# Hybrid decoder layer on one core: up products with a 512-column moving operand, retention in plain fp32, the residual brought to token layout by VectorE and HBM

## The chip, the cores and the metric

The kernel runs on one core of a Trainium2 chip. The metric is device time in microseconds, from start to end of one execution. Inputs lie in HBM in float32; the weights alone are some 200 MB, and each of them is read once. The core has TensorE (PE, with its weight loads listed apart as PEld), VectorE (DVE), ScalarE (ACT), GpSimd (POOL) and SyncE (SP), whose queue issues nearly all DMAs.

## The reference

One layer works on 272 tokens (16 learned ones ahead of 256 of the input) with 2048 features:

```python
u = rmsnorm(h, attn_norm)
aq, ak, av, rq, rk, rv, rg = split(u @ w_in)      # 48 blocks of 128 columns
ya = rmsnorm(diff_attention(aq, ak, av))          # 8 heads
yr = rmsnorm(retention(rq, rk, rv)) * silu(rg)    # 4 heads, head size 256
h = h + concat(ya, yr) @ w_out                    # 16 blocks of 128
u = rmsnorm(h, ffn_norm)
g = u @ w_gate                                    # 44 blocks of 128
h = h + (silu(conv3(g)) * (u @ w_up)) @ w_down    # causal convolution over 3 tokens
out = rmsnorm(h, final_norm)[16:]
```

Retention here is, for each head, a masked and decayed score matrix times the values: `y = (q k^T * decay) v`. All of it is wanted to about float32 accuracy.

## The kernel before

**Layout.** Up to the last product, activations are kept transposed: features on the 128 partitions, tokens along the free axis. A product takes a 128x128 block of a weight matrix as the stationary operand and the tokens of one feature block as the moving operand; 16 feature blocks add up in one PSUM bank.

**High and low parts.** TensorE reads fp32r operands at reduced precision, so each float32 operand is kept as two fp32r tiles: the rounded high part and the rest. A product is three matmuls per block (lines 276 to 278): weight high with activation high, weight high with activation low, weight low with activation high. Each has its own weight load.

**Stages, in order.** A start stage does the first 4 column blocks of `w_in`; then come the other 44 (`gemm`, L257), with attention and retention tasks put between their matmuls by `pump`; then 16 blocks of `w_out` (loop at L550); then 44 pairs of gate and up blocks (loop at L587); then `w_down`, where the roles change: activations are stationary and 512 columns of the weight are the moving operand (L629 to L631). A gate block has 258 tokens (two more for the convolution), an up block 256.

**Weights.** `ahead` (L103) runs before each half block. `load` (L85) issues a 1 MB DMA on the SP queue into one of 3 `raw` tiles; `prep` (L90) makes the high part of half a block on ACT (L99) and the low part on DVE (L100), into 3 buffers each. A load waits until the block three places back has been prepared.

**Order.** The program is written in the order of the text, and a planner that simulates a timeline puts each engine's instructions in its own order. Each engine's queue, and each DMA queue, then runs strictly in that order.

**Retention** (`ret_tasks`, L401). `scores` (L415) multiplies k by q in plain fp32 (L420; one fp32 matmul shows as two records), applies the decay (L422), and splits the result into `sd` and `sl` (L423, L424). `vtr` (L428) transposes the values and splits them into `vh` and `vl` (L434, L435). `av` (L439) makes, for each of 2 value halves and 3 key blocks, three fp32r matmuls (L448 to L450) with 258, 172 and 86 columns.

**The w_out stage** (L550 to L574). For each block j a part of x is loaded (`xres`, L553), added to the product (`hT`, L556), squared and summed (L561, L562), and weighted and split into `ghi` and `glo` (L563, L564) for the next stage. `htr` (L567) brings `hT` to token layout for the residual of the last stage: two TensorE transposes (L570) into PSUM and one copy by ACT (L571) into `htok`.

**The gate and up stage** (L587 to L606). Gate: scale by `rstd2` (L590), convolve on DVE (L592, L595), SiLU on ACT (L598). Up: scale by `rstd2` (L601), multiply with the gate (L602), split into `fhi` (L603) and `flo` (L604). At its end POOL issues the load of `fn` (L611), which DVE scales once (L616), and three more buffers for weight halves are taken from the tiles of the activations (L608, L609).

Of the kernel before, what the change touches and what calls it, by code (L numbers as in the profile page):

```python
# [10 lines left out]
F32 = mybir.dt.float32  # L11
F32R = mybir.dt.float32r
# [7 lines left out]
P = 128  # L20
# [23 lines left out]
class Halves:  # L44
    def __init__(self, tiles):
        self.tiles = tiles

    def __getitem__(self, ix):
        p, k = ix[0], ix[1]
        return self.tiles[k // HK][(p, k % HK) + tuple(ix[2:])]  # L50
# [3 lines left out]
def trunk_kernel(ctx, tc, a, out):  # L54
# [6 lines left out]
    sp = ctx.enter_context(tc.tile_pool(name="small", bufs=2))  # L61

    xhi = Halves([big.tile([P, HK, T], F32R, tag=f"acthi{i}", name=f"xhi{i}")
                  for i in range(2)])
    xlo = big.tile([P, KT, T], F32R, tag="actlo", name="xlo")
# [191 lines left out]
    def gemm(idx, hi, lo, t0, n, pumps):  # L257
        if idx < 4:
            return first[idx]
        if idx < 6:  # L260
            ps = misc(f"mm{idx}")
        elif idx == 6:
            ps = psx[:, 1]
        else:
            ps = ps1.tile([P, 512], F32, tag="mm", bufs=3, name=f"mm{idx}")
        for half in range(2):
            hf = 2 * idx + half
            ahead(hf)
            whi, wlo = pairs.pop(hf)
            for kk in range(HK):  # L270
                k = half * HK + kk
                wh = whi[:, kk * P:(kk + 1) * P]
                wl = wlo[:, kk * P:(kk + 1) * P]
                xh = hi[:, k, t0:t0 + n]
                xl = lo[:, k, t0:t0 + n]
                PE.matmul(ps[:, :n], wh, xh, start=(k == 0), stop=False)  # L276
                PE.matmul(ps[:, :n], wh, xl, start=False, stop=False)  # L277
                PE.matmul(ps[:, :n], wl, xh, start=False, stop=(k == KT - 1))  # L278
                if kk == HK // 2 - 1 or kk == HK - 1:
                    pump(pumps)  # L280
        return ps

    with ExitStack() as p1:
# [118 lines left out]
        def ret_tasks(r, k, q, vs):  # L402
# [4 lines left out]
            sd = [ap_.tile([P, (3 - j) * QT], F32R, tag=f"at{j}", name=f"sd{r}_{j}")  # L407
                  for j in range(3)]
            sl = [ap_.tile([P, (3 - j) * QT], F32R, tag=f"sl{j}", name=f"sl{r}_{j}")
                  for j in range(3)]  # L410
            vh = ap_.tile([P, 3, 2 * P], F32R, tag="q2", name=f"rvh{r}")
            vl = ap_.tile([P, 3, 2 * P], F32R, tag="k2", name=f"rvl{r}")
            st = {}

            def scores(j):  # L415
                def f():
# [4 lines left out]
                    t = ap_.tile([P, NQ], F32, tag="kl", name=f"sdf{r}_{j}")  # L421
                    V.tensor_tensor(out=t[:e - b, :n], in0=ps[:e - b, :n], in1=dk[j], op=ALU.mult)  # L422
                    S.copy(out=sd[j][:e - b], in_=t[:e - b, :n])  # L423
                    V.tensor_tensor(out=sl[j][:e - b], in0=t[:e - b, :n],  # L424
                                    in1=sd[j][:e - b].bitcast(F32), op=ALU.subtract)
                return f

            def vtr(j):  # L428
                def f():
                    b, e = KB[j]  # L430
                    ps = misc(f"rv{r}_{j}")
                    for c in range(2):
                        PE.transpose(ps[:e - b, c * P:(c + 1) * P], vs[c][:, b:e], idt)
                    S.copy(out=vh[:e - b, j], in_=ps[:e - b, :2 * P])  # L434
                    V.tensor_tensor(out=vl[:e - b, j], in0=ps[:e - b, :2 * P],  # L435
                                    in1=vh[:e - b, j].bitcast(F32), op=ALU.subtract)
                return f

            def av(c):  # L439
                def f():  # L440
# [4 lines left out]
                    for j, (b, e) in enumerate(KB):  # L445
                        n = e - b
                        o = y[:, c, j * QT:NQ]
                        PE.matmul(o, vh[:n, j, cs], sd[j][:n], start=(j == 0), stop=False)  # L448
                        PE.matmul(o, vh[:n, j, cs], sl[j][:n], start=False, stop=False)
                        PE.matmul(o, vl[:n, j, cs], sd[j][:n], start=False, stop=(j == 2))  # L450
# [69 lines left out]
        for kind, r in RSEQ:  # L520
# [16 lines left out]
            for c in range(2):  # L537
# [8 lines left out]
        ghi = Halves([big.tile([P, HK, NQ], F32R, tag=f"acthi{i}", name=f"ghi{i}")  # L546
                      for i in range(2)])
        glo = big.tile([P, KT, NQ], F32R, tag="actlo", name="glo")
        htok = big.tile([P, 2, D], F32, tag="htok", name="htok")
        acc2 = yp.tile([P, NQ], F32, name="acc2")  # L550
        for j in range(KT):
# [15 lines left out]
            def htr(j=j, hT=hT):  # L567
                ps = misc(f"ph{j}")
                for m in range(2):
                    PE.transpose(ps[:, m * P:(m + 1) * P], hT[:, 2 + m * P:2 + (m + 1) * P], idt)  # L570
                S.copy(out=htok[:, :, j * P:(j + 1) * P],  # L571
                       in_=ps[:, :2 * P].rearrange("p (m c) -> p m c", m=2))
            side.append(htr)
# [8 lines left out]
    with ExitStack() as p2:  # L582
        fp = p2.enter_context(tc.tile_pool(name="ff", bufs=1))
        fw = p2.enter_context(tc.tile_pool(name="fw", bufs=2))
        fhi = fp.tile([P, NF, SEQ], F32R, name="fhi")
        flo = fp.tile([P, NF, SEQ], F32R, name="flo")
        for f in range(NF):  # L587
            ps = gemm(idx, ghi, glo, 0, NQ, 0)
# [10 lines left out]
            ps = gemm(idx + 1, ghi, glo, 2, SEQ, 0)  # L599
            u = fw.tile([P, SEQ], F32, tag="u", name=f"fu{f}")  # L600
            V.tensor_tensor(out=u, in0=ps[:, :SEQ], in1=rstd2[:, 2:], op=ALU.mult)  # L601
# [194 lines left out]
```

## Time and profile before

| | us |
|---|---|
| Median of 3 runs (1190.66 to 1190.87) | 1190.8 |
| The profiled execution, its own time | 1190.21 |
| Its span in the trace | 1188.4 |
| PE busy | 1176.3 (99%) |
| DVE busy | 788.5 (66%) |
| ACT busy | 559.4 (47%) |
| 16 DMA engines, mean share of the SP queue's packets | 50.8% |

The profile covers one execution. A row of a timeline gives start and length in us, engine, line, operation and operands; matmuls are pipelined, so the length of one (0.28 us) is its latency, and the distance between two starts is what it costs. Windows give busy time per stretch, the granted TensorE clock (1.00 is the 2.4 GHz level) and the busy share of the DMA engines.

### The profile page before, as it was taken

What the parts mean: (1) busy time and instruction counts of PE and PEld (TensorE: products, weight loads), DVE (VectorE), ACT (ScalarE), POOL (GpSimd) and SP (SyncE); (2) the same over time, 40 slices, a digit from 0 to 9 for tenths busy, and PEclk for the clock granted to TensorE, in tenths of its full rate; (3) what the DMA queues carried; (4) which work ended last, traced back from release to release, by engine and by line L of the source; (5) the groups of instructions that cost most, each with busy time, mean ns of one, the idle gap of its engine ahead of it and who ended that gap; (6) DMA issues with size and microseconds to landing.
All of it is one profiled execution on the core that took longest, in us unless ns stands there. A gap on an engine that the chain in (4) does not pass through costs nothing.

```text
span 1188.4 us, 21369 instructions
## 1 busy us (share of the span) xinstructions
PE 1176.3 (99%) x8847; PEld 1129.8 (95%) x8847; DVE 788.5 (66%) x1413; ACT 559.4 (47%) x871; POOL 2.0 (0%) x7
## 2 busy tenths in 40 slices
PE   9999999999999999999999999999999999999997
PEld 8999999999999999999999999999999988888886
DVE  7888877677776567666666666666666645454544
ACT  7576665544445544444444444444444434343442
POOL 0000000000000000000000000000000000000000
PEclk9999999999999999999999999999999999999998
DMA  8544444444446555555555555455555654555552
GB/s 300 205 156 144 142 145 168 163 156 151 168 150 213 198 187 180 190 192 185 178 180 184 193 190 178 178 184 191 193 179 177 218 207 177 200 189 186 195 188 105
DMA packets 35970, 215.72 MB, mean 182 GB/s; under 512 B 4322, under 2 KB 8650, under 8 KB 11168
## 3 DMA queue, kind: packets, MB, share of 16 engines
q1 hardware_dynamic: 35584, 213.17, 50.8%
q8 instruction: 69, 1.13, 0.4%
q0 software_dynamic: 144, 1.05, 0.3%
q14 instruction: 29, 0.24, 0.1%
q10 hardware_dynamic: 144, 0.14, 0.0%
HBM read 212.24 MB, written 2.10 MB: 180 GB/s over the span
## 4 chain that ended last, share of the span: by engine, by line
PE 95%; DMA 2%; DVE 2%; issue 0%; ACT 0%; SPq 0%; DVEq 0%; ACTq 0%
PE mm L276 24%; PE mm L278 23%; PE mm L277 23%; PE o L631 7%; PE o L629 7%; PE o L630 7%; DMA raw<-in_w_in_dram 2%; PE po L380 1%; DVE wlo L100 1%; DMA raw<-in_w_first_dram 1%; PE sc L330 0%; PE sc L328 0%; DMA xr<-in_x_dram 0%; PE pa L368 0%; PE rs L420 0%
## 5 line engine op out<-in xcount | busy, mean ns | idle before, releaser
L99 ACT CAST whi<-raw 128x1024 fp32r<-128x1024 f32 x381 | 399.7, 1049 | 545.5 <-PE mm L277 300.0
L100 DVE TENSOR_TENSOR wlo<-raw,whi 128x1024 fp32r<-128x1024 f32 x381 | 466.1, 1224 | 267.8 <-ACT whi L99 264.7
L276 PE MATMUL mm<-ghi,whi 128*128 128x258 f32 (+1 forms) x1408 | 396.9, 282 | 0.0
L278 PE MATMUL mm<-ghi,wlo 128*128 128x258 f32 (+1 forms) x1408 | 396.6, 282 | 0.0
L277 PE MATMUL mm<-glo,whi 128*128 128x258 f32 (+1 forms) x1408 | 396.1, 281 | 0.0
L277 PEld LDWEIGHTS mm<-glo,whi 128*128 128x128 f32 x1408 | 266.4, 189 | 0.0
L276 PEld LDWEIGHTS mm<-ghi,whi 128*128 128x128 f32 x1408 | 266.0, 189 | 0.0
L278 PEld LDWEIGHTS mm<-ghi,wlo 128*128 128x128 f32 x1408 | 265.8, 189 | 0.0
L276 PE MATMUL mm<-xhi,whi 128*128 128x272 f32 (+1 forms) x688 | 200.4, 291 | 0.0
L277 PE MATMUL mm<-xlo,whi 128*128 128x272 f32 (+1 forms) x688 | 198.9, 289 | 0.0
L278 PE MATMUL mm<-xhi,wlo 128*128 128x272 f32 (+1 forms) x688 | 197.9, 288 | 0.5 <-DVE wlo L100 0.5
L631 PE MATMUL o<-whi,flo 128*128 128x512 f32 x334 | 131.2, 393 | 0.0
L630 PE MATMUL o<-wlo,fhi 128*128 128x512 f32 x334 | 130.3, 390 | 0.0
L278 PEld LDWEIGHTS mm<-xhi,wlo 128*128 128x128 f32 x688 | 129.5, 188 | 0.8 <-DVE wlo L100 0.7
L276 PEld LDWEIGHTS mm<-xhi,whi 128*128 128x128 f32 x688 | 129.6, 188 | 0.1
L277 PEld LDWEIGHTS mm<-xlo,whi 128*128 128x128 f32 x688 | 129.6, 188 | 0.1
L629 PE MATMUL o<-whi,fhi 128*128 128x512 f32 x334 | 117.8, 391 | 0.0
L630 PEld LDWEIGHTS o<-wlo,fhi 128*128 128x128 f32 x334 | 62.7, 188 | 14.2
L631 PEld LDWEIGHTS o<-whi,flo 128*128 128x128 f32 x334 | 62.7, 188 | 13.5
L629 PEld LDWEIGHTS o<-whi,fhi 128*128 128x128 f32 x334 | 62.7, 188 | 13.1
L276 PE MATMUL mm<-yhi,whi 128*128 128x258 f32 x256 | 73.2, 288 | 0.4 <-ACT whi L99 0.4
L278 PE MATMUL mm<-yhi,wlo 128*128 128x258 f32 x256 | 72.3, 284 | 0.0
(245 smaller groups left out, 1086.5 us busy)
## 6 DMA issues: line engine op xcount, KB each, us to landing
raw<-in_w_in_dram SPq DMA_DIRECT2D x44, 1024.0 KB, 4.9
raw<-in_w_gate_dram SPq DMA_DIRECT2D x44, 1024.0 KB, 4.8
raw<-in_w_up_dram SPq DMA_DIRECT2D x44, 1024.0 KB, 4.8
raw<-in_w_down_dram SPq DMA_DIRECT2D x44, 1024.0 KB, 4.9
raw<-in_w_out_dram SPq DMA_DIRECT2D x16, 1024.0 KB, 4.9
raw<-in_w_first_dram SPq DMA_DIRECT2D x6, 512.0 KB, 8.2
xres<-in_x_dram SPq DMA_DIRECT2D x16, 129.0 KB, 3.9
xr<-in_x_dram SPq DMA_DIRECT2D x6, 273.0 KB, 7.4
```

Source lines behind the costliest of these rows:

```text
L99: S.copy(out=hi, in_=src)
L100: V.tensor_tensor(out=lo, in0=src, in1=hi.bitcast(F32), op=ALU.subtract)
L276: PE.matmul(ps[:, :n], wh, xh, start=(k == 0), stop=False)
L277: PE.matmul(ps[:, :n], wh, xl, start=False, stop=False)
L278: PE.matmul(ps[:, :n], wl, xh, start=False, stop=(k == KT - 1))
L380: PE.matmul(ps[:QT, i * P:(i + 1) * P], at[j][:n, i - j], vt[:n, j], start=(j == 0), stop=(j == i))
L629: PE.matmul(o, ah, wh, start=start and kk == 0, stop=False)
L630: PE.matmul(o, ah, wl, start=False, stop=False)
L631: PE.matmul(o, al, wh, start=False, stop=stop and kk == 1)
```

## The change

It has five parts. **Up products:** high and low activations now lie in one tile (`gs`, and `xs` for the first stage), so that one matmul takes both as 2 x 256 columns; the products with the low activations land in the upper half of the PSUM bank and are added afterwards, by an ACT copy of that half and a DVE addition. The factor `rstd2` is put on the gate instead. **Retention:** scores and values stay float32, one plain fp32 matmul in place of three. **Residual:** in place of `htr`, DVE transposes `hT` in 32x32 blocks, and four DMAs per block write the rest of the permutation into an HBM scratch `hd`. **Reading it back:** at f = 8 and f = 16 of the gate and up stage, 1 MB each comes back into `htok`. **Tiles:** `fn` has a pool of its own that opens when the gate and up stage's work tiles are closed.

```diff
-    xhi = Halves([big.tile([P, HK, T], F32R, tag=f"acthi{i}", name=f"xhi{i}")
-                  for i in range(2)])
-    xlo = big.tile([P, KT, T], F32R, tag="actlo", name="xlo")
+    dp = ctx.enter_context(tc.tile_pool(name="dram", bufs=1, space=bass.MemoryType.DRAM))
+
+    xs = [big.tile([P, 2, HK, T], F32R, tag=f"act{i}", name=f"x{i}") for i in range(2)]
+    xhi, xlo = Halves(xs, (0,)), Halves(xs, (1,))
...
-    def gemm(idx, hi, lo, t0, n, pumps):
+    def gemm(idx, hi, lo, t0, n, pumps, both=None):
...
-                PE.matmul(ps[:, :n], wh, xh, start=(k == 0), stop=False)
-                PE.matmul(ps[:, :n], wh, xl, start=False, stop=False)
-                PE.matmul(ps[:, :n], wl, xh, start=False, stop=(k == KT - 1))
+                if both is not None:
+                    xb = both[k // HK][:, :, k % HK, t0:t0 + n]
+                    if k == KT - 1:
+                        PE.matmul(ps[:, :n], wl, xh, start=False, stop=False)
+                    PE.matmul(ps[:, :2 * n], wh, xb, start=(k == 0), stop=(k == KT - 1))
+                    if k < KT - 1:
+                        PE.matmul(ps[:, :n], wl, xh, start=False, stop=False)
+                else:
+                    PE.matmul(ps[:, :n], wh, xh, start=(k == 0), stop=False)
+                    PE.matmul(ps[:, :n], wh, xl, start=False, stop=False)
+                    PE.matmul(ps[:, :n], wl, xh, start=False, stop=(k == KT - 1))
...
-                    t = ap_.tile([P, NQ], F32, tag="kl", name=f"sdf{r}_{j}")
-                    V.tensor_tensor(out=t[:e - b, :n], in0=ps[:e - b, :n], in1=dk[j], op=ALU.mult)
-                    S.copy(out=sd[j][:e - b], in_=t[:e - b, :n])
-                    V.tensor_tensor(out=sl[j][:e - b], in0=t[:e - b, :n],
-                                    in1=sd[j][:e - b].bitcast(F32), op=ALU.subtract)
+                    V.tensor_tensor(out=sd[j][:e - b], in0=ps[:e - b, :n], in1=dk[j],
+                                    op=ALU.mult)
...
-                    S.copy(out=vh[:e - b, j], in_=ps[:e - b, :2 * P])
-                    V.tensor_tensor(out=vl[:e - b, j], in0=ps[:e - b, :2 * P],
-                                    in1=vh[:e - b, j].bitcast(F32), op=ALU.subtract)
+                    S.copy(out=vt[:e - b, j], in_=ps[:e - b, :2 * P])
...
-                        PE.matmul(o, vh[:n, j, cs], sd[j][:n], start=(j == 0), stop=False)
-                        PE.matmul(o, vh[:n, j, cs], sl[j][:n], start=False, stop=False)
-                        PE.matmul(o, vl[:n, j, cs], sd[j][:n], start=False, stop=(j == 2))
+                        PE.matmul(o, vt[:n, j, cs], sd[j][:n], start=(j == 0), stop=(j == 2))
...
-            def htr(j=j, hT=hT):
-                ps = misc(f"ph{j}")
-                for m in range(2):
-                    PE.transpose(ps[:, m * P:(m + 1) * P], hT[:, 2 + m * P:2 + (m + 1) * P], idt)
-                S.copy(out=htok[:, :, j * P:(j + 1) * P],
-                       in_=ps[:, :2 * P].rearrange("p (m c) -> p m c", m=2))
-            side.append(htr)
+            hb = ap_.tile([P, SEQ], F32, tag="t", name=f"hb{j}")
+            V.transpose(out=hb, in_=hT[:, 2:])
+            for i in range(4):
+                c = j * P + i * 32
+                nc.sync.dma_start(
+                    out=hd[:, c:c + 32].rearrange("(b t) f -> t b f", t=32),
+                    in_=hb[i * 32:(i + 1) * 32].rearrange("t (b f) -> t b f", f=32))
...
+            if f in (8, 16):
+                m = f // 8 - 1
+                nc.sync.dma_start(out=htok[:, m], in_=hd[m * P:(m + 1) * P])
...
-            ps = gemm(idx + 1, ghi, glo, 2, SEQ, 0)
+            V.tensor_tensor(out=s, in0=s, in1=rstd2[:, 2:], op=ALU.mult)
+            ps = gemm(idx + 1, ghi, glo, 2, SEQ, 0, gs)
+            ul = fw.tile([P, SEQ], F32, tag="ul", name=f"ful{f}")
+            S.copy(out=ul, in_=ps[:, SEQ:])
             u = fw.tile([P, SEQ], F32, tag="u", name=f"fu{f}")
-            V.tensor_tensor(out=u, in0=ps[:, :SEQ], in1=rstd2[:, 2:], op=ALU.mult)
+            V.tensor_tensor(out=u, in0=ps[:, :SEQ], in1=ul, op=ALU.add)
...
-        fn = big.tile([P, D], F32, tag="acthi0", name="fn")
-        endt = big.tile([P, D], F32R, tag="acthi1", name="endt")
-        tailt = big.tile([P, 2 * D], F32R, tag="actlo", name="tailt")
+        p3.close()
+        fnp = p2.enter_context(tc.tile_pool(name="fnp", bufs=1))
+        fn = fnp.tile([P, D], F32, name="fn")
+        endt = big.tile([P, D], F32R, tag="act0", name="endt")
+        tailt = big.tile([P, 2 * D], F32R, tag="act1", name="tailt")
```

Each of the four DMAs per block writes 256 pieces of 128 B (32 features of one token), whose places in `hd` lie 8 KB apart.

## Rows read from the trace of the kernel before

**Rows 1.** The page, busy time by engine: us, share of the span, instructions

```profile
PE 1176.3 (99%) x8847; PEld 1129.8 (95%) x8847; DVE 788.5 (66%) x1413; ACT 559.4 (47%) x871; POOL 2.0 (0%) x7
```

**Rows 2.** The page, chain that ended last, by engine

```profile
PE 95%; DMA 2%; DVE 2%; issue 0%; ACT 0%; SPq 0%; DVEq 0%; ACTq 0%
```

**Rows 3.** Windows: w_out, gate/up, down, last stores; per stretch engines, PEclk, DMA, GB/s

```profile
361.00:433.00 72.00, 72.00 (x602) 72.00 (x601) 43.34 (x60) 37.06 (x60) 0.00 (x0) 1.00 0.55 196
452.00:934.00 482.00, 482.00 (x4045) 482.00 (x4044) 323.75 (x469) 208.07 (x255) 0.00 (x0) 1.00 0.52 184
944.00:1160.00 216.00, 216.00 (x945) 177.24 (x944) 105.98 (x95) 89.34 (x94) 0.00 (x0) 1.00 0.55 192
1184.00:1186.00 2.00, 0.00 (x0) 0.00 (x0) 0.00 (x0) 0.00 (x0) 0.00 (x0) 0.50 1.03 378
```

**Rows 4.** Timeline of PE: first matmuls of an up, a gate, an up block

```profile
588.90 0.28 PE L276 MATMUL mm<-ghi,whi 128*128 128x256 f32 x1
...
594.60 0.28 PE L276 MATMUL mm<-ghi,whi 128*128 128x258 f32 x1
...
600.35 0.28 PE L276 MATMUL mm<-ghi,whi 128*128 128x256 f32 x1
```

**Rows 5.** Timeline of PE in the down stage, 13 matmuls from first to last

```profile
999.81 0.39 PE L629 MATMUL o<-whi,fhi 128*128 128x512 f32 x1
...
1002.79 0.39 PE L630 MATMUL o<-wlo,fhi 128*128 128x512 f32 x1
```

**Rows 6.** Timeline of the SP queue in the w_out stage, ten raw loads

```profile
361.01 0.33 SPq L87 DMA_DIRECT2D raw<-in_w_out_dram  x1
...
366.98 0.33 SPq L87 DMA_DIRECT2D raw<-in_w_out_dram  x1
...
415.03 0.33 SPq L87 DMA_DIRECT2D raw<-in_w_gate_dram  x1
```

**Rows 7.** Timeline of PEld: two weight loads of `av` with 86 columns

```profile
244.95 0.19 PEld L448 LDWEIGHTS ro<-sd,rvh 86*128 86x128 f32 x1
245.07 0.19 PEld L449 LDWEIGHTS ro<-sl,rvh 86*128 86x128 f32 x1
```

**Rows 8.** Chain in order of time: plain fp32 products of 258, 172, 86 columns

```profile
283.97 0.43 PE rs L420 x2
...
285.92 0.29 PE rs L420 x2
...
287.74 0.15 PE rs L420 x2
```

**Rows 9.** Groups by line: operations added or removed on DVE and ACT

```profile
L601 DVE TENSOR_TENSOR fu<-mm,rstd 128x256 f32<-128x256 f32 x44 | 18.7, 424 | 28.2 <-PE mm L278 28.2
L571 ACT COPY htok<-ph 128x256 f32<-128x256 f32 x16 | 5.7, 365 | 0.2 <-PE ph L570 0.2
```

**Rows 10.** Timelines of ACT and DVE in an up block

```profile
594.73 1.05 ACT L99 CAST whi<-raw 128x1024 fp32r<-128x1024 f32 x1 [1.53 <-issue]
...
595.81 1.22 DVE L100 TENSOR_TENSOR wlo<-raw,whi 128x1024 fp32r<-128x1024 f32 x1
```

**Rows 11.** Timelines of ACT (first and last of five casts) and DVE, w_out stage

```profile
361.74 1.05 ACT L99 CAST whi<-raw 128x1024 fp32r<-128x1024 f32 x1 [1.46 <-PE mm L277]
...
373.74 1.05 ACT L99 CAST whi<-raw 128x1024 fp32r<-128x1024 f32 x1 [1.77 <-issue]
...
364.30 0.48 DVE L564 SCALAR_TENSOR_TENSOR glo<-hT,c_ffn_norm,ghi 128x258 fp32r<-128x258 f32 x1
```

**Rows 12.** The page, DMA issues: KB each, median us to landing

```profile
raw<-in_w_out_dram SPq DMA_DIRECT2D x16, 1024.0 KB, 4.9
```

**Rows 13.** Timeline of DVE at the change to the down stage

```profile
940.35 0.42 DVE L604 TENSOR_TENSOR flo<-fu,fhi 128x256 fp32r<-128x256 f32 x1
942.75 1.23 DVE L616 TENSOR_SCALAR fn<-fn 128x2048 f32<-128x2048 f32 x1 [1.99 <-DMA fn<-in_final_norm_dram]
```

More of the change, by code (lines that the diff above doesn't have):

```diff
@@ L44, with __init__ @@
 class Halves:
-    def __init__(self, tiles):
+    def __init__(self, tiles, lead=()):
         self.tiles = tiles
+        self.lead = lead
     def __getitem__(self, ix):
         p, k = ix[0], ix[1]
-        return self.tiles[k // HK][(p, k % HK) + tuple(ix[2:])]
+        return self.tiles[k // HK][(p,) + self.lead + (k % HK,) + tuple(ix[2:])]
 @with_exitstack
@@ L406, in ret_tasks @@
             dk = [dt_[:KB[0][1], 0], dt_[:QT, 1, :2 * QT], dt_[:QT, 1, 2 * QT:]]
-            sd = [ap_.tile([P, (3 - j) * QT], F32R, tag=f"at{j}", name=f"sd{r}_{j}")
+            sd = [ap_.tile([P, (3 - j) * QT], F32, tag=f"at{j}", name=f"sd{r}_{j}")
                   for j in range(3)]
[L409 to L412, printed above, removed]
+            vt = ap_.tile([P, 3, 2 * P], F32, tag="q2", name=f"rvt{r}")
             st = {}
@@ L544, in trunk_kernel @@
         pump(len(side))
[L546 to L549, printed above, removed]
+        gs = [big.tile([P, 2, HK, NQ], F32R, tag=f"act{i}", name=f"g{i}") for i in range(2)]
+        ghi, glo = Halves(gs, (0,)), Halves(gs, (1,))
+        hd = dp.tile([SEQ, D], F32, name="hd")
         acc2 = yp.tile([P, NQ], F32, name="acc2")
@@ L583, in trunk_kernel @@
         fp = p2.enter_context(tc.tile_pool(name="ff", bufs=1))
-        fw = p2.enter_context(tc.tile_pool(name="fw", bufs=2))
+        htok = big.tile([P, 2, D], F32, tag="htok", name="htok")
         fhi = fp.tile([P, NF, SEQ], F32R, name="fhi")
         flo = fp.tile([P, NF, SEQ], F32R, name="flo")
+        p3 = ExitStack()
+        fw = p3.enter_context(tc.tile_pool(name="fw", bufs=2))
         for f in range(NF):
+            if f in (8, 16):
+                m = f // 8 - 1
+                nc.sync.dma_start(out=htok[:, m], in_=hd[m * P:(m + 1) * P])
             ps = gemm(idx, ghi, glo, 0, NQ, 0)
```

## The prediction

> **What bounds the kernel now.** I read the busy times first, then the chain that ended last, then windows over the stages, then single timelines where a part of the change lies. PE is busy for 1176.3 of 1188.4 us, DVE for 66% and ACT for 47% [rows 1], and PE makes 95% of the chain that ended last [rows 2]. In the windows PE is busy for the whole of the w_out stretch, of the gate and up stretch and of the down stretch, at a granted clock of 1.00, the 2.4 GHz level, while the DMA engines are busy for 0.52 to 0.55 of them [rows 3]. So time is won by what PE need no longer do, and lost only by what makes PE wait. The unit of price is the distance between starts of matmuls. An up block's 48 matmuls take 594.60 - 588.90 = 5.70 us, 118.75 ns each; a gate block's 48 take 5.75 us, 119.8 ns each [rows 4]. In the down stage 13 steps take 2.98 us, 229.2 ns each, at 512 columns [rows 5].
>
> **Up products.** Per feature block three matmuls of 256 columns (3 x 118.75 = 356.3 ns) become one of 512 and one of 256 (229.2 + 118.75 = 348.0 ns): the columns stay, one instruction and one weight load go. That is 8.3 ns, times 16 feature blocks, times 44 up blocks: 5.85 us. The 229.2 ns come from a moving operand that is one run, where the new one is two runs of 256; no row shows that form. Bounds: nothing gained if 512 columns take 2 x 118.75 ns; and 8.5 us if the whole of an instruction's excess over its columns goes (118.75 ns less 256 columns at 2.4 GHz, 106.7 ns, is 12.1 ns, times 704). I take 5.85, from the row with the same number of columns.
>
> The trace shows an excess of 12.1 ns at 256 columns and, with 213.3 ns for 512 columns, of 15.9 ns there [rows 4, 5]. The Trainium skill ("TensorE: Matmul & The Clock Gate", section "Wait — 56ns, not 53.3ns?") puts the distance at N / 2.4 GHz plus about 2.5 ns; by that this part would give 704 x 2.5 ns, an estimate of 1.8 us. The trace doesn't agree, at 12.1 ns, and the sum goes by the rows.
>
> What up blocks get in exchange lies on ACT and DVE: the copy of the upper half (0.37 us by the nearest copy out of PSUM) and one more DVE operation (0.42) per pair of blocks [rows 9], 16 us on ACT and 19 us on DVE over 44. DVE was busy for 323.75 of 482 us of this stretch and would be for 343, ACT for 208 and then 224 [rows 3]; both stay under PE. The copy waits for the last up matmul, and the DVE addition for the copy; queued behind the addition on DVE is the low part of a later half of weights. ACT may be in a weight cast of 1.05 us when the up block ends, so the addition can be late by 1.05 + 0.37 = 1.4 us. The low part that starts at 595.81 and ends 1.22 us later [rows 10] belongs to a half that PE reaches two halves after 594.60, at the next block's end, 600.35 [rows 4]: 3.3 us to spare. Likewise the new factor on the gate waits for ACT's SiLU, at most one cast, 1.05 us. I take nothing for both.
>
> **Residual.** Between the raw loads of the w_out stage, which follow PE's pace, nine periods last 415.03 - 361.01 = 54.02 us, 6.00 each [rows 6]. The 48 matmuls of 258 columns take 5.75 of it [rows 4], so two transposes take 0.25 us. Without them 16 x 0.25 = 4.0 us go. With them goes ACT's copy of 0.37 us per block [rows 9], which frees ACT alone. The DVE transpose of 128x256 has no row; between nothing and three times the nearest operation of that shape (0.42, [rows 9]) I take 0.42: DVE is busy for 43.3 of 72 us here [rows 3], so even 16 x 1.3 us fits.
>
> The four DMAs per block are new on SP's queue: 4 x 0.33 = 1.3 us of issue. They wait for the transpose. `glo`, after which DVE is free for it, ends at 364.78 [rows 11]; then 0.42 of transpose and 1.3 of issue end at 366.5, and the next raw load, queued behind, was issued at 366.98 [rows 6]. So that load is not late by the issue, and if the order of the queue is worse, by some 1 to 3 us. There is room: the load of 361.01 lands 4.9 us later [rows 12], at 365.9; the five casts from 361.74 on are those of the two halves of two earlier blocks and then its own first, at 373.74 [rows 11]. That leaves 7.8 us. That cast starts as PE begins a half, and its weights are wanted two halves later, 6.0 us; cast and low part take 1.05 + 1.22, so 3.7 us more. A stream of loads may fall behind by 11.5 us before PE waits.
>
> **The packets of these DMAs** are the unknown. Per block and DMA engine they are 4 x 256 / 16 = 64 pieces of 128 B, and some 4 completions: 68. Raw and x loads keep the engines busy for 0.55 x 6.00 = 3.3 us of a period [rows 3]; without transposes the period is 5.75 us, so 2.45 us are free, 36 ns per packet. With 11.5 us of credit over 16 periods (0.72 each) it is 47 ns. The nearest rows are the last stores, whose rows have 1 to 1.5 KB and lie 8 KB apart too: 378 GB/s at a share of 1.03 [rows 3] is 22.9 GB/s per engine, 45 ns for 1 KB. By bytes alone 128 B would take 5.6 ns. From below the bound is 5.6 ns, from above nothing in the trace, as it has no store so short; I take 45 ns, the shortest packet that a row shows, since what a packet costs apart from its bytes isn't known. At 45 ns the engines need 3.3 + 3.06 = 6.36 us of 5.75, 16 x 0.61 = 9.8 us in all, inside the credit: no cost.
>
> **Retention.** Old weight loads follow each other at 0.12 us even beside 86 columns [rows 7], so a triple takes 3 x 0.12 = 0.36 us at 258 columns and some 0.35 at 172 and 86: 1.05 per value half. Plain fp32 takes 0.43, 0.29 and 0.15 us for these columns [rows 8]; at 86 two weight loads of 128 columns may bind (0.23), I take 0.20. That is 0.92, a gain of 0.13 us, times 8: 1.0 us, bounds 0.8 and 1.4. DVE and ACT lose 24 and 12 small operations, off the chain.
>
> **Reading back, tiles.** Two loads of 1 MB (4.9 us, [rows 12]) at f = 8 and 16 put the next raw load back by about 3 us of engine time, inside 7.8; nothing. The load of `fn` on POOL's queue waited for the last convolution and now waits for `flo`, which ends at 940.77; DVE was already waiting 1.99 us for it before L616 [rows 13]. Queued behind L616 are low parts. If the planner keeps its place, DVE waits some 5 us longer, of which the 3.3 us above are hidden: 0 to 2 us, I take 0, as the planner sees when the tile becomes free.
>
> **Sum.** 5.85 + 4.0 + 1.0 = 10.85 us. The profiled execution took 1190.2 us (span 1188.4, and 1.8 around it), 0.6 below the median of 1190.8. So 1179.4 for it, and 1180.0 against the median. Its own bounds: 8.5 + 4.0 + 1.4 gives 1177, and 0 + 4.0 + 0.8 with 2 us for `fn` gives 1188; some 1 us either way is for waits of the first 50 us, which the planner may move.
>
> **Rivals.**
> 1. **The 128 B stores take over** (slower). Place: the w_out stage's DMA engines, with raw loads behind the stores on one queue. It decides from 3.3 + 68 t > 5.75 + 0.72 on, t = 47 ns, and cancels the gain at t = 57 ns (16 x (3.3 + 3.88 - 5.75) - 11.5 = 11.4 us). For it: the credit is used up almost wholly at 45 ns already. Against: bytes are an eighth of the 1 KB rows'. Taking a short store as two passes of the shortest row shown, 90 ns, the stage needs 3.3 + 6.1 = 9.4 us per block: 16 x 3.67 - 11.5 = 47 us of waiting, 1227 us. Chance 0.17. The Trainium skill ("DMA: Bandwidth & Descriptors", section "Specifications") says that transfers under 512 B make the DMA engine read, modify and write, which would speak for this rival; no row here shows such a store.
> 2. **Stores partly over the credit**, t of 47 to 57 ns: 1181 to 1190 us. Chance 0.06.
> 3. **The wide matmul gains nothing**, since two runs of 256 cost what two matmuls did: 1190.8 - 5.0 = 1186 us. For it: no row has the form. Against: columns alone set the distance from 256 to 512 within 16 ns. Chance 0.08.
> 4. **DVE's new waits reach PE**: the addition behind ACT makes weights late by more than 3.3 us. If that happened in each pair by 0.5 us, 22 us would be lost: 1202. Against: 1.4 us is the most that a cast can add. Chance 0.04.
>
> **How the numbers follow.** The forecast has 0.65, and 1180.0 is its time. A measurement of this kernel tells about 0.2% (2.4 us) from no change. Faster: 0.65 + 0.08 and most of rival 2, 0.78. Within 0.2%: the end of rival 2 and the start of rival 1, 0.04. Slower: the rest of rivals 1 and 4, 0.18. The range starts at 1176 (the gain's bound and the 1 us) and ends at 1193, which takes in rivals 2 and 3 and the start of 1; what lies above is rivals 1 and 4, under 0.2.
>
> **What would show it.** Up blocks of 5.57 us in the timeline of PE, with 348 ns from one 512-column matmul to the next; raw loads of the w_out stage 5.75 us apart; PE busy for all of that stage's window with a DMA share near 0.9; ACT's casts not waiting for raw loads. Wrong it would be if raw loads of that stage land more than 7.8 us late, PE shows idle time before L276 or L278 released by ACT or DVE there or in the up blocks, or the wide matmuls start over 237 ns apart from what follows.

## The result, and the profile after

The changed kernel takes 1182.7 us (median of four executions, 1182.0 to 1185.1) where the kernel before takes 1190.7 beside it: ratio 0.9937, interval 0.9925 to 0.9949. The same kernel run again in the first batch of experiments gave 1182.4, ratio 0.9928 [0.9916, 0.9941]. So it is faster by 8.0 and 8.5 us in the two comparisons; forecast were 10.85 us less, 1180.0. The profiled execution of the change was the slowest of its four, 1185.1 us with a span of 1183.3.

Its page shows what [rows 1] and [rows 2] showed of before: 760 instructions fewer on PE, which is still busy for 99% of the span and still makes nearly the whole of the chain. The last two lines are from its list of DMA issues (KB each, median us to landing):

```profile
PE 1169.6 (99%) x8087; PEld 1091.6 (92%) x8087; DVE 803.9 (68%) x1449; ACT 563.9 (48%) x887; POOL 2.0 (0%) x7
...
PE 94%; DMA 3%; DVE 2%; issue 0%; SPq 0%; ACT 0%; DVEq 0%; ACTq 0%
...
raw<-in_w_out_dram SPq DMA_DIRECT2D x16, 1024.0 KB, 5.2
...
hd<-hb SPq DMA_DIRECT2D x64, 32.0 KB, 3.6
```

Windows of it over a stretch of the start, the beginning of w_out, w_out, and gate/up (busy time of PE, PEld, DVE, ACT, POOL; granted clock; DMA share; GB/s):

```profile
16.00:18.00 2.00, 2.00 (x11) 2.00 (x11) 2.00 (x3) 2.00 (x4) 0.00 (x0) 0.50 1.04 403
...
344.00:361.00 17.00, 16.10 (x130) 15.47 (x128) 12.49 (x22) 7.91 (x13) 0.00 (x0) 1.00 0.43 118
361.00:433.00 72.00, 72.00 (x602) 72.00 (x601) 51.06 (x77) 34.95 (x49) 0.00 (x0) 1.00 0.81 247
452.00:934.00 482.00, 482.00 (x3391) 451.96 (x3390) 340.41 (x514) 220.62 (x301) 0.00 (x0) 1.00 0.52 186
```

Beside [rows 3]: PE stays full through w_out and gate/up, DVE rises from 43.3 to 51.1 us in w_out and from 323.8 to 340.4 in gate/up (343 foretold), and w_out's DMA share goes from 0.55 to 0.81. The first two stretches are taken up with the experiments.

The timeline of PE has the new pairs and the lengths of an up and a gate block, beside [rows 4]:

```profile
587.22 0.39 PE L281 MATMUL mm<-g,whi 128*128 128x512 f32 x1
587.45 0.28 PE L283 MATMUL mm<-g,wlo 128*128 128x256 f32 x1
...
592.84 0.28 PE L285 MATMUL mm<-g,whi 128*128 128x258 f32 x1
...
598.58 0.39 PE L281 MATMUL mm<-g,whi 128*128 128x512 f32 x1
```

An up block takes 592.84 - 587.22 = 5.62 us (5.70 before, 5.57 foretold), a gate block 5.74. Over the 39 up and 39 gate blocks that start from 460 to 900 us the means are 5.617 and 5.737, against 5.702 and 5.745 before (39 and 38 blocks). From each start to the next, wide matmuls take 232.4 ns and narrow ones 118.6 in the mean, 351.0 a pair.

Where the time went is read from the stages' first matmuls. First before, then the change run again (the first score product of retention, the first product of w_out, of gate/up, of down):

```profile
234.31 0.61 PE L420 MATMUL rs<-rq,rk 128*100 128x258 f32 x2
...
336.94 0.28 PE L276 MATMUL mm<-yhi,whi 128*128 128x258 f32 x1
...
433.68 0.28 PE L276 MATMUL mm<-ghi,whi 128*128 128x258 f32 x1
...
938.00 0.40 PE L629 MATMUL o<-whi,fhi 128*128 128x512 f32 x1
```

```profile
235.52 0.61 PE L426 MATMUL rs<-rq,rk 128*100 128x258 f32 x2
...
337.47 0.28 PE L285 MATMUL mm<-yhi,whi 128*128 128x258 f32 x1
...
431.47 0.28 PE L285 MATMUL mm<-g,whi 128*128 128x258 f32 x1
...
931.48 0.61 PE L637 MATMUL o<-whi,fhi 128*128 128x512 f32 x2
```

With spans of 1188.4 and 1181.3 us: the stretch up to the first `rs` +1.2, retention 102.63 to 101.95 (-0.7), w_out 96.74 to 94.00 (-2.7), gate/up 504.32 to 500.01 (-4.3), down with the end 250.4 to 249.9 (-0.6); in sum -7.1 us of span.

### The profile page after: what moved, and what is told of

Same layout as the page of the kernel before. It is cut to its first block, busy times and chain, and to the rows that moved or that the text cites. A ratio compares the mean times of both kernels' runs of the same rounds, so it can differ in the third digit from the quotient of the medians.

```text
span 1183.3 us, 19959 instructions
## 1 busy us (share of the span) xinstructions
PE 1169.6 (99%) x8087; PEld 1091.6 (92%) x8087; DVE 803.9 (68%) x1449; ACT 563.9 (48%) x887; POOL 2.0 (0%) x7
## 3 DMA queue, kind: packets, MB, share of 16 engines
q0 software_dynamic: 144, 1.05, 0.3%
## 4 chain that ended last, share of the span: by engine, by line
PE 94%; DMA 3%; DVE 2%; issue 0%; SPq 0%; ACT 0%; DVEq 0%; ACTq 0%
PE mm L285 17%; PE mm L286 16%; PE mm L287 16%; PE mm L281 14%; PE o L639 7%; PE mm L283 7%; PE o L637 7%; PE o L638 7%; DMA raw<-in_w_first_dram 1%; PE po L389 1%; DMA raw<-in_w_in_dram 1%; DVE wlo L101 1%; PE ro L449 1%; PE mm L280 0%; PE sc L339 0%; PE sc L337 0%
## 5 line engine op out<-in xcount | busy, mean ns | idle before, releaser
L281 PE MATMUL mm<-g,whi 128*128 128x512 f32 x704 | 250.8, 395 | 0.0
L285 PE MATMUL mm<-x,whi 128*128 128x272 f32 (+1 forms) x688 | 200.5, 292 | 0.0
L285 PE MATMUL mm<-g,whi 128*128 128x258 f32 x704 | 199.2, 283 | 0.0
L287 PE MATMUL mm<-x,wlo 128*128 128x272 f32 (+1 forms) x688 | 197.9, 288 | 1.2 <-DVE wlo L101 1.2
L286 PE MATMUL mm<-x,whi 128*128 128x272 f32 (+1 forms) x688 | 198.7, 289 | 0.0
L286 PE MATMUL mm<-g,whi 128*128 128x258 f32 x704 | 198.1, 281 | 0.0
L287 PE MATMUL mm<-g,wlo 128*128 128x258 f32 x704 | 198.0, 281 | 0.0
L283 PE MATMUL mm<-g,wlo 128*128 128x256 f32 x660 | 185.4, 281 | 0.0
L281 PEld LDWEIGHTS mm<-g,whi 128*128 128x128 f32 x704 | 132.6, 188 | 27.2
L286 PEld LDWEIGHTS mm<-g,whi 128*128 128x128 f32 x704 | 133.4, 190 | 1.8
L287 PEld LDWEIGHTS mm<-g,wlo 128*128 128x128 f32 x704 | 132.8, 189 | 0.0
L285 PEld LDWEIGHTS mm<-g,whi 128*128 128x128 f32 x704 | 132.6, 188 | 0.0
L287 PEld LDWEIGHTS mm<-x,wlo 128*128 128x128 f32 x688 | 129.5, 188 | 1.5 <-DVE wlo L101 1.4
L285 PEld LDWEIGHTS mm<-x,whi 128*128 128x128 f32 x688 | 129.6, 188 | 0.1
L286 PEld LDWEIGHTS mm<-x,whi 128*128 128x128 f32 x688 | 129.6, 188 | 0.1
L283 PEld LDWEIGHTS mm<-g,wlo 128*128 128x128 f32 x660 | 124.6, 189 | 0.0
```

The lines of the kernel that those rows point to most:

```text
L281: PE.matmul(ps[:, :2 * n], wh, xb, start=(k == 0), stop=(k == KT - 1))
L283: PE.matmul(ps[:, :n], wl, xh, start=False, stop=False)
```

## The experiments

**The change once more, and its parts undone one at a time.** The first run has no edit.

> The changed kernel once more, nothing edited. Theory (chance): in its profile one early DMA landed late, PE then idled 1.54 us and ran some 4.5 us at the lower clock, so its first 45 us were 2.4 us longer; a new profile without that shows the first L285 matmul into psx at about 43.4 us after the span's start, as before, and 1.00 as granted clock of the first 30 us, and the times spread over about 1181.9 to 1185. Rival (layout): the one tile for high and low activations makes the start slower every time; then that matmul stands at 45 to 46 us again and the times stay near 1183.

1182.36 us (1182.29 to 1183.14), ratio 0.9928 [0.9916, 0.9941]. In the profiled execution of the first comparison PE waited 1.5 us in one piece for a cast, up to 13.70 us, and after that its granted clock stands at 0.50, the 1.2 GHz level, from 16 to 18 us (the window above). Here two waits share 1.4 us, the longest of 0.8, and the clock stays at 1.00. The order of the instructions is the same in both, so those 2 us belong to that execution. The product into `psx` that the expectation names starts at 44.1 us, nearer the theory's 43.4 than the rival's 45 to 46.

`no_wide` takes the up products back to three matmuls of 256 columns, in the new layout of the activations:

```diff
-            V.tensor_tensor(out=s, in0=s, in1=rstd2[:, 2:], op=ALU.mult)
-            ps = gemm(idx + 1, ghi, glo, 2, SEQ, 0, gs)
-            ul = fw.tile([P, SEQ], F32, tag="ul", name=f"ful{f}")
-            S.copy(out=ul, in_=ps[:, SEQ:])
+            ps = gemm(idx + 1, ghi, glo, 2, SEQ, 0)
...
-            V.tensor_tensor(out=u, in0=ps[:, :SEQ], in1=ul, op=ALU.add)
+            V.tensor_tensor(out=u, in0=ps[:, :SEQ], in1=rstd2[:, 2:], op=ALU.mult)
```

> Only the up products are put back to three matmuls with rstd2 applied behind them; all else as changed. Theory: the wide matmul is worth what the gate and up stage shows, 504.3 us before and 500.0 after from its first matmul to the first of the down stage, so 4.3 us: about 1187.0, and that stage at 504 us. Rival: the prediction's 5.85 us are there and something else in the stage eats 1.5 of them, then undoing it costs 5.9: 1188.6. Rival: the stage gained by something else than the wide matmul, then nothing changes: 1182.7.

1187.88 us, ratio 0.9973 [0.9962, 0.9983]: the wide form is worth 5.5 us. The timeline of PE (first matmuls of an up, a gate, an up block):

```profile
586.57 0.28 PE L285 MATMUL mm<-g,whi 128*128 128x256 f32 x1
...
592.27 0.28 PE L285 MATMUL mm<-g,whi 128*128 128x258 f32 x1
...
598.05 0.28 PE L285 MATMUL mm<-g,whi 128*128 128x256 f32 x1
```

The up block is back at 5.70 us (mean 5.700), which accounts for 44 x 0.083 = 3.7 us. The other 1.6 us lie in the gate blocks, whose code isn't touched: 5.773 us against 5.737. Neither theory had foreseen that.

`ret_split` takes retention back to the triples of split values, with the lines of the kernel before.

```diff
...
-                        PE.matmul(o, vt[:n, j, cs], sd[j][:n], start=(j == 0), stop=(j == 2))
+                        PE.matmul(o, vh[:n, j, cs], sd[j][:n], start=(j == 0), stop=False)
+                        PE.matmul(o, vh[:n, j, cs], sl[j][:n], start=False, stop=False)
+                        PE.matmul(o, vl[:n, j, cs], sd[j][:n], start=False, stop=(j == 2))
```

> Only retention is put back to split values and three matmuls; all else as changed. Theory: plain fp32 gives 0.8 us on PE (the stretch from the first score product to the first w_out product went from 102.6 to 101.8 us): about 1183.5. Rival: fewer small operations on DVE and ACT mattered too, 1184.5 or more. Rival: nothing, 1182.7.

1183.17 us, ratio 0.9936 [0.9923, 0.9950]; the medians are 0.8 us apart, and the retention stage is 102.63 us long, as before. The timeline of PE has the old triples, the first of nine, and the product behind them:

```profile
269.94 0.28 PE L457 MATMUL ro<-sd,rvh 100*128 100x258 f32 x1
...
270.89 0.37 PE L285 MATMUL mm<-x,whi 128*128 128x272 f32 x1
```

and that of the changed kernel the plain products that stand for them (one row for the six records), and the next product:

```profile
269.42 1.08 PE L449 MATMUL ro<-sd,rvt 100*128 100x258 f32 x6
270.29 0.37 PE L285 MATMUL mm<-x,whi 128*128 128x258 f32 x1
```

From the first start to that of the next product, nine old matmuls take 270.89 - 269.94 = 0.95 us (1.05 foretold), the plain ones 270.29 - 269.42 = 0.87 (0.92 foretold). So a value half gives 0.08 us and not 0.13. Summed from start to next start over all eight halves, some of which other products divide, it is 7.24 us in `ret_split` and 6.61 in `again`: 0.63 of the 0.7 us.

`htr` takes the residual back to TensorE's transposes, without the scratch.

```diff
-            hb = ap_.tile([P, SEQ], F32, tag="t", name=f"hb{j}")
-            V.transpose(out=hb, in_=hT[:, 2:])
...
+            def htr(j=j, hT=hT):
+                ps = misc(f"ph{j}")
...
+                    PE.transpose(ps[:, m * P:(m + 1) * P], hT[:, 2 + m * P:2 + (m + 1) * P], idt)
```

> Only the residual is put back to TensorE transposes and an ACT copy; no HBM scratch, no load back. Theory: the 32 transposes cost PE 16 x 0.24 us = 3.8 us, and the 0.9 us of PE idle at the start of the w_out stage, where it was 0.44 us before, belongs to the scratch stores, so undoing costs 3.3: about 1186.0, with idle of PE between 344 and 361 us back at about 0.45. Rival: the idle there has another cause (retention's end), stays near 0.9, and undoing costs 3.8: 1186.5. Rival: the stores cost what the transposes did, 1182.7.

1186.03 us, ratio 0.9956 [0.9943, 0.9968]: the scratch is worth 3.7 us. w_out takes 96.81 us here against 94.0, and its beginning has less idle time on PE, 0.44 us against 0.90 above. The gate/up stage is 0.3 us longer than in the change run again, and the stretch from the first `w_down` product to the end 0.5 us, all of it behind the last matmul. A window of its beginning of w_out:

```profile
344.00:361.00 17.00, 16.56 (x137) 16.20 (x136) 10.91 (x16) 9.71 (x17) 0.00 (x0) 1.00 0.52 186
```

The three parts undone give 5.5 + 0.8 + 3.7 = 10.0 us, 1.6 more than the whole change; as much lies in the gate blocks of `no_wide`.

**Where the packets' limit lies.** The prediction's largest doubt was the price of a 128 B packet. In the SP queue of the changed kernel raw loads now follow each other at 5.77 us (375.36 to 433.03 in ten periods), with the four stores in between:

```profile
375.36 0.35 SPq L88 DMA_DIRECT2D raw<-in_w_out_dram  x1
377.57 1.83 SPq L569 DMA_DIRECT2D hd<-hb  x4
381.13 0.35 SPq L88 DMA_DIRECT2D raw<-in_w_out_dram  x1
...
433.03 0.35 SPq L88 DMA_DIRECT2D raw<-in_w_up_dram  x1
```

The trace's records of DMA packets give the price directly: in these ten periods 11,223 packets of 128 B take 13 ns each, not 45, so 68 packets take 0.9 us of a period. (By shares, 0.81 of 5.77 us less the 3.3 of the other loads, the expectations below took 20 ns; but the window of 0.81 holds more raw loads than periods.) Two runs load this part more. `p32` cuts the stores into pieces of 32 B:

```diff
-        hd = dp.tile([SEQ, D], F32, name="hd")
+        hd = dp.tile([32, 32, D // 4], F32, name="hd")
...
-                    out=hd[:, c:c + 32].rearrange("(b t) f -> t b f", t=32),
-                    in_=hb[i * 32:(i + 1) * 32].rearrange("t (b f) -> t b f", f=32))
+                    out=hd[:, :, c // 4:c // 4 + 8].rearrange("q t f -> t q f"),
+                    in_=hb[i * 32:(i + 1) * 32].rearrange("t (q f) -> t q f", f=8))
...
```

> The scratch stores go in pieces of 32 bytes instead of 128, 256 data packets per block and engine instead of 64 (the residual's places in the scratch are thereby permuted). Theory (a small packet has a price of its own, about 20 ns as the DMA share of the w_out stage gives it): the period's transfers are 3.3 + 260 x 0.020 = 8.5 us against 5.77, so w_out becomes bound by its loads after the credit of 11.5 us is spent: 16 x 2.7 - 11.5 = 32 us more, 1214 us, and the raw w_out loads 8 us or more apart. Rival 1 (the price follows the bytes): no change, 1182.4 us and a period of 5.77. Rival 2 (45 ns, the prediction's value): 16 x (3.3 + 11.7 - 5.8) - 11.5 = 136 us more, 1318 us.

1190.7 us (ten executions, 1188.2 to 1192.0), ratio 0.9998 [0.9989, 1.0007]: 8.3 us more than the change, which none of the three gave. Its SP queue:

```profile
352.53 4.89 SPq L569 DMA_DIRECT2D hd<-hb  x8
...
394.25 5.11 SPq L569 DMA_DIRECT2D hd<-hb  x4
```

Here SP's queue has no room left. The issue of four stores takes 5 us and more, and with the other two issues a period is 6.5 us (ten periods from 367.14 to 432.13), with a share of 0.87 on the DMA engines. But a quarter of that isn't the price of an issue: the first eight stores take 0.61 each, and later one of four, mostly the third, stands in issue for about 3 us by itself:

```profile
395.51 3.24 SPq L569 DMA_DIRECT2D hd<-hb  x1
```

What holds it, the engines' backlog or the queue, is not shown. The loss is 5.4 us in w_out and 3.2 in the gate/up stage; PE waits mostly for low parts. The packets of 32 B take 8.2 ns in the mean of their records; the share gives (0.87 x 6.5 - 3.3) / 260 = 9.

`twice` keeps the pieces and doubles their number:

```diff
+        hd2 = dp.tile([SEQ, D], F32, name="hd2")
...
-            for i in range(4):
+            for i, dst in [(i, dst) for dst in (hd2, hd) for i in range(4)]:
...
-                    out=hd[:, c:c + 32].rearrange("(b t) f -> t b f", t=32),
+                    out=dst[:, c:c + 32].rearrange("(b t) f -> t b f", t=32),
```

> Each residual block is stored twice, into a second scratch tensor that nobody reads: 8 stores per block, 136 packets of 128 bytes per period and engine instead of 68. Theory (18 to 20 ns a packet): 3.3 + 136 x 0.018 to 0.020 = 5.8 to 6.0 us of transfers in a period of 5.77, at most 0.2 x 16 = 3.8 us, which the credit of 11.5 us covers: 1182.4 us, within 1, and a DMA share of 0.95 or more from 361 to 433 us. SP's issues, 8 x 0.46 + 0.70 = 4.4 us, fit too. Rival (45 ns, the prediction's value): 3.3 + 6.1 = 9.4 us, 16 x 3.6 - 11.5 = 46 us more, 1229 us.

1194.5 us (1191.7 to 1196.0), ratio 1.0022 [1.0009, 1.0035]: 12 us more than the change, and again neither. Its SP queue, then windows:

```profile
351.69 13.37 SPq L570 DMA_DIRECT2D hd<-hb  x24
365.15 0.39 SPq L88 DMA_DIRECT2D raw<-in_w_out_dram  x1
...
403.33 0.35 SPq L88 DMA_DIRECT2D raw<-in_w_out_dram  x1
...
409.34 0.40 SPq L88 DMA_DIRECT2D raw<-in_w_out_dram  x1
```

```profile
361.00:381.00 20.00, 20.00 (x168) 20.00 (x168) 14.11 (x22) 9.78 (x15) 0.00 (x0) 1.00 0.89 281
```

```profile
350.00:365.00 15.00, 14.11 (x113) 13.48 (x113) 11.38 (x20) 8.02 (x13) 0.00 (x0) 1.00 0.37 67
361.00:381.00 20.00, 14.79 (x99) 14.34 (x98) 7.88 (x12) 5.73 (x8) 0.00 (x0) 0.83 0.76 241
```

The first of the windows is the change run again, the others `twice`. Three blocks' stores, 24 of them, stand in a row on SP's queue, and the raw load behind them is issued at 365.15; the DMA engines' share is 0.37 meanwhile. PE runs out of weights (its longest wait for a cast there is 4.5 us), and the granted clock falls to 0.83 over the stretch. So it was SP's queue, and not the DMA engines, that starved PE. After that the period is 6.0 us or more with a DMA share of about 0.8, but from 381 to 433 us PE waits for nothing. A store's issue still takes about 0.46 us, as the expectation had it; what it left out is a wait (waits of the SP queue from 340 to 436 us: total, times, longest):

```profile
SPq L570 <- DMA raw<-in_w_out_dram: 10.7, 10, 2.1
```

In the trace SP's DMAs signal eight semaphores in turn, and each is issued only when the one eight places before it has landed. With ten DMAs to a period, a store, which doesn't use the weights, so stands behind the landing of the period's raw load, for 0.7 to 1.2 us each time from 390 us on.

By the Trainium skill ("DMA: Bandwidth & Descriptors", section "Specifications") transfers under 512 B make the engine read, modify and write. What that costs here is inside 13 ns for 128 B and 8.2 ns for 32 B; no run shows it apart.

**The start of the kernel.** `sub_first` issues one small load earlier:

```diff
+    sub = const("attn_subln", [P, 1])
     idt = const("ident", [P, P])
...
-    sub = const("attn_subln", [P, 1])
```

> The load of attn_subln is issued ahead of the identity and the alibi table; nothing else changes. Theory (the start stage is set by what lands late: DVE's wait for this load, 0.5 to 3.3 us in the runs, holds 0.5 to 1.5 us of PE at about 55 us): DVE's wait is gone, PE waits 0 to 0.4 us there, 1181.4 us and the runs closer together. Rival (the cover of PE there is lost to DVE's own work, 27 to 58 us being full on DVE, and the load only names the wait): the wait moves to another releaser, 1182.4 us.

1182.48 us (1182.03 to 1184.07), ratio 0.9935 [0.9922, 0.9947]. The wait has gone: between 30 and 120 us PE waited 1.0 us for a low part in `again` and waits for nothing here, and DVE no longer waits for the load. That execution's span is 0.9 us shorter. But the medians, 1182.4 and 1182.5, don't show it, so no gain is claimed.

**The beginning of w_out.** `hb_task` hands the transposes and stores out in the middle of the next block:

```diff
-            hb = ap_.tile([P, SEQ], F32, tag="t", name=f"hb{j}")
-            V.transpose(out=hb, in_=hT[:, 2:])
+            def put(j=j, hT=hT):
+                hb = ap_.tile([P, SEQ], F32, tag="t", name=f"hb{j}")
+                V.transpose(out=hb, in_=hT[:, 2:])
...
+            side.append(put)
```

> The DVE transposes and the scratch stores become a task that is handed out in the middle of the next block, as the TensorE transposes of before were. Theory (the 0.45 us that PE waits more at the start of w_out comes from two transposes standing on DVE ahead of two low parts): PE idle between 344 and 361 us goes from 0.9 to about 0.45, 1181.9 us. Rival (the wait there is for ScalarE's high parts, which stand behind copies of their own): 0.9 stays, 1182.4 us.

1182.36 us, ratio 0.9937 [0.9924, 0.9949]; PE's waits from 344 to 361 us are unchanged:

```profile
PE mm L285 <- ACT whi L100: 0.7, 2, 0.4
PE mm L287 <- DVE wlo L101: 0.2, 1, 0.2
```

But the run doesn't test the theory, since the planner left the two transposes where they were, ahead of the two low parts (timeline of DVE in `hb_task`):

```profile
351.07 0.76 DVE L567 STREAM_TRANSPOSE hb<-hT 128x256 f32<-128x256 f32 x2
351.75 2.32 DVE L101 TENSOR_TENSOR wlo<-raw,whi 128x1024 fp32r<-128x1024 f32 x2
```

The timelines of PE, in `htr` first and then in the change run again, show where the time goes:

```profile
350.14 0.73 PE L568 MATMUL ph<-c_ident,hT 128*128 128x128 f32 x4
...
351.55 0.39 PE L285 MATMUL mm<-yhi,whi 128*128 128x258 f32 x1 [0.44 <-ACT whi L100]
```

```profile
352.40 0.39 PE L285 MATMUL mm<-yhi,whi 128*128 128x258 f32 x1 [0.30 <-ACT whi L100]
```

PE waits 0.44 us for ScalarE's second cast in both. Of the other 0.46 us, 0.30 are a wait for the first cast, in a place where `htr` has four TensorE transposes to do, and 0.16 one for a low part behind the DVE transposes. That is read from the order of the rows; no run took it apart.

**Why a wide matmul takes 232 ns and not 229.** `contig` lays the high and low columns of a K-tile side by side, so that the wide operand is one run:

```diff
-                    xb = both[k // HK][:, :, k % HK, t0:t0 + n]
+                    xb = both[k // HK][:, k % HK, t0:t0 + 2 * n]
...
-        gs = [big.tile([P, 2, HK, NQ], F32R, tag=f"act{i}", name=f"g{i}") for i in range(2)]
+        gs = [big.tile([P, HK, 2 * NQ], F32R, tag=f"act{i}", name=f"g{i}") for i in range(2)]
...
```

> The gate/up stage's activations lie with high and low part of a K-tile in one run of 512 columns (258 and 258 side by side), so that the wide matmul reads one run instead of two runs 8 KB apart; the low activations are thereby taken two tokens off, the work is the same. Theory (the two runs cost something): the wide matmul goes from 232.8 ns to the 229 ns of the down stage's 512 columns, 3.8 ns x 704 = 2.7 us, 1179.7 us; up blocks from 5.62 to about 5.56 us. Rival (the 3.6 ns belong to a wide matmul between two narrow ones, each with its own weights): 1182.4 us, within 0.5, and up blocks stay at 5.62 us.

1184.0 us (1183.6 to 1185.5), ratio 0.9946 [0.9934, 0.9959]: slower, which neither had. The wide matmuls stay at 233.0 ns (232.4 in the change; mean distance to the next start), the narrow ones rise from 118.6 to 121.3. Up blocks take 5.669 us, gate blocks 5.718; 44 x (0.052 - 0.019) = 1.5 us, nearly the whole difference. Two runs are not the cause.

`two` puts wide matmuls beside wide ones:

```diff
...
                     PE.matmul(ps[:, :2 * n], wh, xb, start=(k == 0), stop=(k == KT - 1))
-                    if k < KT - 1:
+                    if kk % 2 and k < KT - 1:
+                        PE.matmul(ps[:, :n], wp_, xp_, start=False, stop=False)
                         PE.matmul(ps[:, :n], wl, xh, start=False, stop=False)
+                    wp_, xp_ = wl, xh
...
```

> In the up products two wide matmuls follow each other and then their two narrow ones (wide k, wide k+1, narrow k, narrow k+1) in place of wide and narrow in turn; the same products. Theory (a wide matmul that stands between narrow ones takes 233 ns, one beside another wide one 229, as the down stage's do): one of two changes of width goes, 1.9 ns a pair x 704 = 1.3 us, up blocks from 5.617 to 5.587, 1181.1 us. Rival (a wide matmul in this stage costs 233 ns whatever stands beside it, as a 256-column one costs 118: the surcharge grows with the columns): up blocks stay within 0.01 of 5.617, 1182.4 us.

1183.57 us, ratio 0.9936 [0.9922, 0.9949]. The timeline of PE (first matmuls of an up, a gate, an up block):

```profile
585.04 0.63 PE L282 MATMUL mm<-g,whi 128*128 128x512 f32 x2
...
590.65 0.28 PE L288 MATMUL mm<-g,whi 128*128 128x258 f32 x1
...
596.42 0.63 PE L282 MATMUL mm<-g,whi 128*128 128x512 f32 x2
```

Up blocks stay at 5.61 us (mean 5.606) and two wide matmuls in a row take 466 ns, 233 each: the rival holds for them. Gate blocks went to 5.774 us, 44 x 0.037 = 1.6 us, though nothing in them changed.

`align` gives the rows of the gate/up activations 272 columns:

```diff
-        gs = [big.tile([P, 2, HK, NQ], F32R, tag=f"act{i}", name=f"g{i}") for i in range(2)]
+        gs = [big.tile([P, 2, HK, T], F32R, tag=f"act{i}", name=f"g{i}") for i in range(2)]
...
-            S.activation(out=ghi[:, j], in_=hT, func=AF.Copy, scale=g2[:, j:j + 1])
+            S.activation(out=ghi[:, j, Q0:], in_=hT, func=AF.Copy, scale=g2[:, j:j + 1])
...
-            ps = gemm(idx + 1, ghi, glo, 2, SEQ, 0, gs)
+            ps = gemm(idx + 1, ghi, glo, Q0 + 2, SEQ, 0, gs)
```

> The rows of the gate/up activations take 272 columns in place of 258, with the 258 in their last columns, so that every up operand begins at a multiple of 64 bytes; before, the rows began 8 bytes further on for each K-tile. Theory (where an operand begins sets the few ns by which the distances of like matmuls differ, 117.6 to 122 ns): up pairs from 351.3 to about 348 ns, up blocks to 5.57, gate blocks to 5.72 or less, 704 x 3 ns + 44 x 0.02 = 3 us, 1179.5 us. Rival (those ns are not the operands' place): both blocks within 0.02, 1182.4 us, within 1.

1179.68 us (1179.21 to 1179.86), ratio 0.9901 [0.9888, 0.9915]: 2.7 us faster than the change. The timeline of PE (first matmuls of an up, a gate, an up block):

```profile
594.48 0.40 PE L281 MATMUL mm<-g,whi 128*128 128x512 f32 x1
...
600.06 0.28 PE L285 MATMUL mm<-g,whi 128*128 128x258 f32 x1
...
605.77 0.40 PE L281 MATMUL mm<-g,whi 128*128 128x512 f32 x1
```

Up blocks take 5.58 us (mean 5.578), gate blocks 5.71 (5.715), wide matmuls 230.2 ns: 44 x (0.039 + 0.022) = 2.7 us, all of the gain. The tile shares its buffer with `xs`, whose rows had 272 columns all along. So the layout of the rows is shown to be the cause. Which property of it acts is not: with the starts, the rows' length and the distance between high and low half changed too. The Trainium skill ("SBUF — State Buffer", section "Specifications (TRN2)") has lines of 16 bytes and a price for crossing into a new one. By that, in the changed kernel, the even K-tiles, whose up operands begin 8 bytes past such a line (counted from the tile's start), should be slower than the odd ones, which begin on one. The trace doesn't agree: the wide matmuls of even and odd K-tiles are 232.5 and 232.3 ns from their successors. Nor does `align` make the K-tiles alike, though all their up operands begin at multiples of 64 bytes: their wide matmuls still take 225.8 to 235.0 ns by K-tile (225.0 to 240.0 in the change).

`align_y` does the same for w_out's activations as well:

```diff
-        yhi = yp.tile([P, KT, NQ], F32R, name="yhi")
-        ylo = yp.tile([P, KT, NQ], F32R, name="ylo")
+        yhi = yp.tile([P, KT, T], F32R, name="yhi")
+        ylo = yp.tile([P, KT, T], F32R, name="ylo")
...
```

> As align, and the rows of w_out's activations too take 272 columns in place of 258, so that each operand of w_out begins at a multiple of 64 bytes (before, 8 bytes further on for each K-tile). Theory (the operands' place): w_out's period goes from 5.77 to about 5.71 us, the gate blocks' 5.715 of align, 16 x 0.055 = 0.9 us on top of align, 1178.8 us. Rival (in w_out other work sets the distances, as in the gate blocks, which moved by 0.02 and by more in kernels that left their operands alone): the period stays at 5.77, 1179.7 us.

1179.36 us (1178.93 to 1179.72), ratio 0.9903 [0.9887, 0.9920], the fastest median, though its runs overlap with those of `align`. Raw loads of w_out follow each other at 5.747 us (366.72 to 406.95 in seven periods) instead of 5.767: 16 x 0.02 = 0.3 us, nearer the rival.

## Why the prediction was right, and where it was off

The forecast's case came true, with the time 2.4 to 2.7 us above it: 8.0 to 8.5 us of gain for 10.85.

- **Up products: the mechanism was right, the term too large.** 5.85 us were foretold from a pair of 348.0 ns. The pair takes 232.4 + 118.6 = 351.0 ns, which over 704 pairs is 3.7 us, and the gate/up stage is 4.3 us shorter (0.4 of it in the gate blocks). The step that failed is the 229.2 ns taken from the down stage: they hold only for some layouts of the moving operand. The text doubted the two runs; `contig` clears these, and with rows of 272 columns the pair takes 230.2 + 118.4 = 348.6 ns, and the time is 1179.7 us. Undone in the new layout the term is 5.5 us, of which 1.6 lie in the gate blocks, about which the prediction said nothing.
- **Residual: 4.0 foretold; w_out became 2.7 to 2.8 us shorter,** 3.7 us by the time of `htr`, with 0.3 us in the gate/up stage and 0.5 behind the last matmul, places that the prediction didn't count. The period went to 5.77 us, not 5.75 (0.3 us over 16 blocks), and PE idles 0.45 us more at the stage's beginning: by the rows, four of the 32 transposes filled a wait for a cast there and were partly free.
- **Packets: no cost, as taken, but with more room.** 13 ns instead of 45. The step was the nearest row, whose packets are long (1.5 and 2 KB in the trace, at 68 and 87 ns, not 1 to 1.5 KB as the text had it). Rival 1 needed 47 ns. SP's queue was priced at 0.33 us an issue and takes 0.46 for a store; in both runs that brought a loss the raw loads stood behind stores in this queue. It was the resource to make a rival of.
- **Retention: 1.0 foretold, 0.7 to 0.8 measured,** at the lower bound: a value half went from 0.95 to 0.87 us and not from 1.05 to 0.92.
- **DVE's new waits, rival 4: none reaches PE,** which waits for nothing from 361 to 940 us. The addition, below, waits for the copy in each pair (groups of DVE operations in the changed kernel; the 0.0 is the idle time ahead of the factor):

```profile
L607 DVE TENSOR_TENSOR fu<-mm,ful 128x256 f32<-128x256 f32 x44 | 18.7, 424 | 29.2 <-ACT ful L605 29.2
...
L602 DVE TENSOR_TENSOR fs<-fs,rstd 128x256 f32<-128x256 f32 x44 | 18.4, 417 | 0.0
...
L566 DVE STREAM_TRANSPOSE hb<-hT 128x256 f32<-128x256 f32 x16 | 7.0, 442 | 0.4
```

  The 29.2 us of waiting over 44 pairs replace the 28.2 that its predecessor waited for PE [rows 9]. The copy takes 0.37 us and the DVE transpose 0.44, as taken.
- **Reading back and `fn`: nothing, as taken,** but not where the text had them: the two loads of the residual are issued together at 439.16 us, ahead of f = 8, and DVE's wait for `fn` is 1.1 us where it was 1.99 [rows 13].
- **Rival 3 is excluded** by the pair of 351.0 against 356.3 ns.

## What to carry to other kernels

Price a wider matmul with a row whose operand lies as the new one will, and when like matmuls differ by 3 ns, try another row length: here 5% more columns of padding gave a third of what the whole change gave. Small stores to HBM are priced twice, on the DMA engines and on the queue that issues them; count the issue time of every store on that queue, what earlier DMA it must see land, and what loads stand behind it. When an edit hands work out elsewhere, look in the trace whether it moved. Sum a change by stages, from the first matmul of one to the first of the next, since a start that varies by 1 to 2 us hides terms of that size in the total.

## What was not expected of the hardware

- A 512-column matmul with new weights takes 232.4 ns from its start to the next one's, or 230.2, by the layout of its operand's rows alone.
- Blocks of identical code and operands take 5.737 us, 5.774 (`two`) or 5.773 (`no_wide`), with other matmuls only in the blocks between them. The cause is open.
- A store's issue on SP takes 0.46 us for 256 pieces and 0.61 for 1024 in the first eight, later about 3 us for one of four; an engine's time per packet was 13 ns at 128 B and 8.2 at 32 B.
